# Hybrid MLA/FoX layer: the query latent's normalising factor applied inside the softmax exponential instead of to the latent

## Chip, core and metric

The kernel runs on one core of one Trainium2 chip. The metric is the device time of one execution in microseconds, as the median of several executions. Less is better.

## The reference, cut to what the change touches

One decoder layer for 512 tokens of width 2048. The layer has two kinds of attention heads; the change concerns only the eight MLA heads, whose queries come out of a normalised latent of 768 channels:

```
def _rms_norm(x, g):
    y = xf * lax.rsqrt(jnp.mean(xf * xf, axis=-1, keepdims=True) + NORM_EPS)
    return y * g
...
proj = _rms_norm(x, g_pre) @ w_in            # q_lat (768), kv_lat (512), k_rope, gates, FoX q/k/v
q = (_rms_norm(q_lat, g_q) @ w_uq)           # 8 heads x (128 nope + 64 rope)
kv = (_rms_norm(kv_lat, g_kv) @ w_ukv)
logits = (qn @ k_nope.T + rope(qr) @ rope(k_rope).T) * MLA_QK_DIM ** -0.5
p = softmax(causal(logits));  o = p @ v
...
x + _rms_norm(concat(o_mla * silu(gate), o_fox * silu(gate)) @ w_out, g_post)
```

The factor `rsqrt(mean(q_lat^2) + eps)` is one number per token, that is, one per row of the logits. It can be multiplied in before the query projection or after the scores; the result is the same up to rounding.

## The kernel before

All arithmetic is float32. A product of two float32 matrices is made of three TensorE matmuls (lines 138 to 140, `mm3`): each operand is split into a high part (ScalarE rounds it to the fast format) and a low part (VectorE subtracts the high part). Weights arrive in chunks of 128x1024 numbers, loaded by SyncE's queue into `raw`; `divide` (lines 241 to 252) splits each into `whi` on ScalarE (L250) and `wlo` on VectorE (L251). For every chunk TensorE therefore waits for a VectorE instruction of its own chunk.

The program is one long list of matmuls on TensorE, and everything else is threaded between them: small work items stand in a list `todo`, and `pump` takes one or two of them after each step of a product. `wait(n)` puts n empty items in the list. The order on each engine is then settled by the scheduler of the framework when the program is built; each engine runs its own list strictly in that order.

The stages, in the order of time: the FoX heads' projections and their attention (to about 405 us); the latents and the gates of the MLA heads, made with sums of weight blocks (to about 600 us; the products are called p1, p4, p2, q6, g5, g7, g3, their outputs in PSUM A, B, C, G, in the profile gl, gm, gc, gd); four pairs of MLA heads (to about 735 us); the output projection with its final normalisation.

**The latents.** The transposed query latent lies in six tiles of 128 channels x 512 tokens (`lat`, indices 0 to 5), the key/value latent in four more (6 to 9). `latent` squares each tile on ScalarE and adds up (L1148, L1152). `latent_stats(j)` sums over the channels with TensorE (L1162, outputs lbq and lbk), and makes the factor of each token as a column of 128x4 numbers (L1167 to L1172). `diagonals` and `latent_row` turn that column into a row that is the same in all partitions: ScalarE and VectorE make diagonal matrices (L452, L453), TensorE multiplies them by ones (L461, L462, outputs lrq and lrk) and VectorE copies the row out (L463, into `ls`). `latent_part(i)` multiplies tile i by the row and by the channel's gain (L1182) and splits the product (L129, L130, outputs `ln`).

**The MLA heads.** For each pair of heads the queries (`mq`) come from the six query latents, the keys and values (`mk`, `mv`) from the four others. The factor 192 ** -0.5 (`SC_M`) is put on the queries when they are split (L1333 to L1336). `Head.scores` makes four blocks of scores per head (`sm`, up to 128x512), adds the causal mask on VectorE (L607), takes the negated row maximum on VectorE (L620, column 0 of `st`), the exponentials on ScalarE with that as bias and the row sum as a second output (L622, output `pm`), and divides by the sum on VectorE (L623, L624). `Head.flip` transposes the blocks on TensorE (L631, `ptm`), splits them (`phm`, `plm`), and `Head.values` multiplies by the values (`pvm`).

Scores and transposes share three PSUM banks (`att_bank`): a new block of scores or transposes waits until the block three before it has been read, for scores by the exponential.

Of the kernel before, what the change touches and what calls it, by code (L numbers as in the profile page):

```python
# [19 lines left out]
P = 128  # L20
# [43 lines left out]
def tile_hybrid_layer(  # L64
# [77 lines left out]
    def newton_rsqrt(y, v, t):  # L142

        dve.tensor_tensor(out=t, in0=y, in1=v, op=ALU.mult)
        dve.tensor_tensor(out=t, in0=t, in1=y, op=ALU.mult)
        dve.tensor_scalar(out=t, in0=t, scalar1=-0.5, scalar2=1.5, op0=ALU.mult, op1=ALU.add)
        dve.tensor_tensor(out=y, in0=y, in1=t, op=ALU.mult)
# [325 lines left out]
    def wait(n):  # L473
        todo.extend([lambda: None] * n)
# [110 lines left out]
    class Head:  # L585
# [7 lines left out]
        def scores(self, b):  # L593
# [27 lines left out]
            p = pp.tile([P, n], F32, tag=f"p{b}", name=f"p{self.name}{b}")  # L621
            act.activation(p, s[:, :n], AF.Exp, bias=st[:, 0:1], accum_out=st[:, 1:2])  # L622
            dve.reciprocal(st[:, 2:3], st[:, 1:2])  # L623
# [516 lines left out]
    def raw(i):  # L1140
        return raws_of[(i // 2 + 1) % 5][:, i % 2, :]
# [11 lines left out]

    lat_diag = {}

    def latent_stats(j):
# [13 lines left out]
        dve.reciprocal(y, w)  # L1170
        newton_rsqrt(y, v, w)
        dve.tensor_tensor(out=y, in0=y, in1=rcol, op=ALU.mult)  # L1172
        lat_diag[j] = diagonals(y, f"lr{name}")
# [6 lines left out]
    def latent_part(i):  # L1180
        j = int(i >= 6)
        dve.scalar_tensor_tensor(  # L1182
            out=raw(i), in0=raw(i), scalar=gcol[:, NK + i : NK + i + 1], in1=accs[:, j, :],
            op0=ALU.mult, op1=ALU.mult,
        )
        latents[i] = split(raw(i), f"ln{i}")
# [109 lines left out]
    for i in range(4, 8):  # L1296
        todo.append(lambda i=i: latent(i, raw(i)))
    wait(2)
    todo.append(lambda: latent_stats(0))
    todo.append(lambda: latent_stats(1))  # L1300
    wait(6)
    todo.append(lambda: latent_row(0))
    todo.append(lambda: latent_row(1))
    wait(3)
    for i in range(10):
        todo.append(lambda i=i: latent_part(i))
# [21 lines left out]
    for p in range(4):  # L1328
# [3 lines left out]
        proj_T(c["q"], [(qb[i], P, cols(i * P)) for i in range(3)], qnh, qnl, rate=2)  # L1332
        q = [[split(qb[i], f"mq{p}{i}", SC_M, first=P)] for i in range(2)]  # L1333
        wholes = slot(f"mw{p}")
        qw = [[whole_block(wholes, i, qb[i], SC_M)] for i in range(2)]
        a, b = rotate(qb[2], P, SC_M, f"q{p}")  # L1336
        for i in range(2):
# [274 lines left out]
```

## Time and profile before

| | us |
|---|---|
| three runs | 909.24, 910.70, 915.02 |
| median of the three | 910.7 |
| the profiled execution, its own time | 909.88 |
| its span, first to last instruction | 908.1 |
| mean granted TensorE clock | 0.998 |

A profile row gives the start and the length in us, the engine, the line of the kernel, the operation with output and inputs by name, its shape, and in brackets the time the engine stood idle before it and what ended that. `x2` means that neighbouring instructions of one kind are merged. PE is TensorE, PEld its weight loads, DVE is VectorE, ACT is ScalarE, SPq is SyncE's queue of DMA issues. The ends of matmuls are modelled and overlap the next one's start, so distances between starts are what to read there.

### The profile page before, as it was taken

What the parts mean: (1) busy time and instruction counts of PE and PEld (TensorE: products, weight loads), DVE (VectorE), ACT (ScalarE), POOL (GpSimd) and SP (SyncE); (2) the same over time, 40 slices, a digit from 0 to 9 for tenths busy, and PEclk for the clock granted to TensorE, in tenths of its full rate; (3) what the DMA queues carried; (4) which work ended last, traced back from release to release, by engine and by line L of the source; (5) the groups of instructions that cost most, each with busy time, mean ns of one, the idle gap of its engine ahead of it and who ended that gap; (6) DMA issues with size and microseconds to landing.
All of it is one profiled execution on the core that took longest, in us unless ns stands there. A gap on an engine that the chain in (4) does not pass through costs nothing.

```text
span 908.1 us, 12914 instructions
## 1 busy us (share of the span) xinstructions
PE 897.0 (99%) x4732; PEld 773.1 (85%) x4732; DVE 634.9 (70%) x1082; ACT 423.5 (47%) x779; POOL 71.7 (8%) x89
## 2 busy tenths in 40 slices
PE   9999999999999999999999999999999999999996
PEld 8988888898889988888998998878888888888885
DVE  3477778437473683474677777978878986997785
ACT  5772434234222342242445556644455465654483
POOL 1010111110120111101000000000100000000021
PEclk9999999999999999999999999999999999999999
DMA  9378897987897987988888875548674146799888
GB/s 299 99 200 218 228 206 207 238 228 187 229 263 199 227 232 204 231 203 215 276 285 306 271 236 163 162 134 205 152 173 127 47 133 196 251 320 303 272 223 249
DMA packets 120195, 195.20 MB, mean 215 GB/s; under 512 B 15906, under 2 KB 59452, under 8 KB 120132
## 3 DMA queue, kind: packets, MB, share of 16 engines
q1 hardware_dynamic: 106052, 158.84, 55.3%
q0 software_dynamic: 13344, 35.13, 20.7%
q8 instruction: 37, 0.61, 0.3%
q10 hardware_dynamic: 736, 0.40, 0.2%
q14 instruction: 26, 0.21, 0.1%
HBM read 182.27 MB, written 62.41 MB: 269 GB/s over the span
## 4 chain that ended last, share of the span: by engine, by line
PE 91%; DVE 4%; DMA 3%; ACT 1%; issue 1%; SPq 0%; ACTq 0%; DVEq 0%
PE fv L562 4%; PE fg L138 3%; PE fq L140 3%; PE fq L138 3%; PE fq L139 3%; PE fg L140 3%; PE fg L139 3%; PE fk L138 3%; PE fk L140 3%; PE fk L139 3%; PE sm L605 3%; PE fv L138 2%; PE fv L140 2%; PE fv L139 2%; PE mq L138 2%; PE mq L140 2%
## 5 line engine op out<-in xcount | busy, mean ns | idle before, releaser
L251 DVE TENSOR_TENSOR wlo<-raw,whi 128x1024 fp32r<-128x1024 f32 (+3 forms) x205 | 242.6, 1186 | 152.5 <-ACT whi L250 148.1
L250 ACT CAST whi<-raw 128x1024 fp32r<-128x1024 f32 (+3 forms) x205 | 209.1, 1022 | 286.9 <-PE fk L139 48.3
L138 PE MATMUL fq<-h,whi 128*128 128x512 f32 x128 | 52.6, 411 | 0.0
L138 PE MATMUL fg<-h,whi 128*128 128x512 f32 x128 | 50.9, 398 | 0.0
L140 PE MATMUL fq<-h,wlo 128*128 128x512 f32 x128 | 50.3, 393 | 0.0
L140 PE MATMUL fg<-h,wlo 128*128 128x512 f32 x128 | 50.2, 392 | 0.0
L139 PE MATMUL fq<-h,whi 128*128 128x512 f32 x128 | 50.1, 391 | 0.0
L138 PE MATMUL fk<-h,whi 128*128 128x512 f32 x128 | 50.0, 391 | 0.0
L139 PE MATMUL fg<-h,whi 128*128 128x512 f32 x128 | 49.9, 390 | 0.0
L139 PE MATMUL fk<-h,whi 128*128 128x512 f32 x128 | 49.8, 389 | 0.0
L140 PE MATMUL fk<-h,wlo 128*128 128x512 f32 x128 | 49.8, 389 | 0.0
L140 PE MATMUL fv<-whi,h 128*128 128x256 f32 (+1 forms) x128 | 39.5, 309 | 0.0
L139 PE MATMUL fv<-wlo,h 128*128 128x256 f32 (+1 forms) x128 | 39.5, 309 | 0.0
L138 PE MATMUL fv<-whi,h 128*128 128x256 f32 (+1 forms) x128 | 39.5, 309 | 0.0
L562 PE MATMUL fv<-whi,h 128*128 128x456 f32 x128 | 37.7, 378 | 0.0
L295 POOL DMA_DIRECT2D t<-t x16 | 13.4, 838 | 290.1 <-DMA t<-in_w_out_dram 261.2
L622 ACT ACTIVATE pf<-sf,stf 128x128 f32<-128x128 f32 (+3 forms) x32 | 16.9, 528 | 27.1 <-DVE stf L620 27.1
L138 PE MATMUL mq<-ln,whi 128*128 128x512 f32 x72 | 28.9, 401 | 0.0
L140 PEld LDWEIGHTS fq<-h,wlo 128*128 128x128 f32 x128 | 24.0, 188 | 5.4
L140 PEld LDWEIGHTS fg<-h,wlo 128*128 128x128 f32 x128 | 24.0, 188 | 5.3
L139 PE MATMUL mq<-ln,whi 128*128 128x512 f32 x72 | 28.3, 393 | 0.0
L140 PEld LDWEIGHTS fk<-h,wlo 128*128 128x128 f32 x128 | 24.0, 188 | 5.0
(525 smaller groups left out, 2460.4 us busy)
## 6 DMA issues: line engine op xcount, KB each, us to landing
raw<-in_w_in_dram SPq DMA_DIRECT2D x80, 512.0 KB
raw<-in_w_out_dram SPq DMA_DIRECT2D x32, 512.0 KB
t<-in_w_out_dram SPq DMA_DIRECT2D x24, 512.0 KB
raw<-t SPq DMA_DIRECT2D x24, 512.0 KB
t<-t POOLq DMA_DIRECT2D x16, 512.0 KB, 7.6
awaymg<-rmg POOLq DMA_DIRECT2D x8, 512.0 KB, 8.3
t<-in_w_out_dram POOLq DMA_DIRECT2D x8, 512.0 KB, 7.9
second<-in_w_in_dram SPq DMA_DIRECT2D x8, 512.0 KB
```

What stands on the lines that cost most here:

```text
L138: pe.matmul(o, ah, bh, start=first, stop=False, **kw)
L139: pe.matmul(o, ah, bl, start=False, stop=False, **kw)
L140: pe.matmul(o, al, bh, start=False, stop=last, **kw)
L250: act.copy(hi[:, :m], raw[:, :m])
L251: dve.tensor_tensor(out=lo[:, :m], in0=raw[:, :m], in1=hi[:, :m].bitcast(F32), op=ALU.subtract)
L295: pool.dma_start(to.rearrange("p (k c) -> p k c", k=2), second, accum_op=ALU.add)
L562: pe.matmul(banks[t][:, :n], a[k][:, tss[t]], b[:, j, :], start=k == 0 and m == 0, stop=k == NK - 1 and m == 2,)
L605: pe.matmul(s[:, :nn], a[:, qs], c[:, :nn], start=(i == 0), stop=(i == len(pairs) - 1))
L622: act.activation(p, s[:, :n], AF.Exp, bias=st[:, 0:1], accum_out=st[:, 1:2])
```

## The change

The row of the query latent, its diagonals and the six multiplications by it are left out. Instead the latent tiles are multiplied by the channel's gain alone while they are split (ScalarE with the gain as a per-partition scale, VectorE with one combined instruction). The factor of each token, times `SC_M`, times the factor of the first normalisation, is kept as a column `qcol` (128x4). The exponential of an MLA block takes the column as its per-partition scale, and the negated maximum is multiplied by it first, in a new ScalarE instruction on 128x1 numbers. `SC_M` disappears from the splitting of the queries. The list of work items is reordered: the six query tiles can be split before any statistics, so they come first, and the key/value latent's statistics come before the query's.

```diff
@@ Head.scores
+            unit = 1.0
+            if self.fox is None:
+                unit = qcol[:, b : b + 1]
+                act.mul(st[:, 0:1], st[:, 0:1], unit)
-            act.activation(p, s[:, :n], AF.Exp, bias=st[:, 0:1], accum_out=st[:, 1:2])
+            act.activation(p, s[:, :n], AF.Exp, bias=st[:, 0:1], scale=unit, accum_out=st[:, 1:2])
@@ latent_stats
+        if j == 0:
+            dve.scalar_tensor_tensor(out=qcol, in0=y, scalar=SC_M, in1=rcol, op0=ALU.mult, op1=ALU.mult)
+            return
         dve.tensor_tensor(out=y, in0=y, in1=rcol, op=ALU.mult)
         lat_diag[j] = diagonals(y, f"lr{name}")
@@ latent_part
+        if j == 0:
+            latents[i] = split(raw(i), f"ln{i}", gcol[:, NK + i : NK + i + 1])
+            return
         dve.scalar_tensor_tensor(
@@ the list of work
-    todo.append(lambda: latent_stats(0))
-    todo.append(lambda: latent_stats(1))
-    wait(6)
-    todo.append(lambda: latent_row(0))
-    todo.append(lambda: latent_row(1))
-    wait(3)
-    for i in range(10):
+    todo.append(lambda: latent_stats(1))
+    for i in range(6):
+        todo.append(lambda i=i: latent_part(i))
+    todo.append(lambda: latent_row(1))
+    todo.append(lambda: latent_stats(0))
+    wait(1)
+    for i in range(6, 10):
         todo.append(lambda i=i: latent_part(i))
@@ the MLA heads
-        q = [[split(qb[i], f"mq{p}{i}", SC_M, first=P)] for i in range(2)]
+        q = [[split(qb[i], f"mq{p}{i}", first=P)] for i in range(2)]
-        qw = [[whole_block(wholes, i, qb[i], SC_M)] for i in range(2)]
-        a, b = rotate(qb[2], P, SC_M, f"q{p}")
+        qw = [[whole_block(wholes, i, qb[i])] for i in range(2)]
+        a, b = rotate(qb[2], P, 1.0, f"q{p}")
```

The change moves instructions at three places that the prediction speaks of.

First, VectorE in the second half of the latents, from the split of a late key/value latent to the low part of the third of the four chunks of the product g3 (`gc` are the gates' tiles, `lat` and `ln` the latents). Before:

```order
L251 TENSOR_TENSOR wlo_5521<-raw_5466,whi_5520 128x1024
L130 TENSOR_TENSOR ln_5505<-lat_4797,ln_5505 128x512
L130 TENSOR_TENSOR ln_5515<-lat_3743,ln_5515 128x512
L1182 SCALAR_TENSOR_TENSOR lat_3743<-lat_3743,gcol,ls 128x512
L251 TENSOR_TENSOR wlo_5543<-raw_5492,whi_5542 128x1024
L130 TENSOR_TENSOR ln_5531<-lat_3743,ln_5531 128x512
L1234 SCALAR_TENSOR_TENSOR gc_4657<-gcm_5210,ncol,gc_4657 128x512
L1234 SCALAR_TENSOR_TENSOR gc_4657<-gcm_5211,ncol,gc_4657 128x512
L1234 SCALAR_TENSOR_TENSOR gc_5463<-gcm_5210,hcol,gc_5463 128x512
L1234 SCALAR_TENSOR_TENSOR gc_5463<-gcm_5211,hcol,gc_5463 128x512
L251 TENSOR_TENSOR wlo_5568<-raw_5518,whi_5567 128x1024
```

The same stretch now, up to the same chunk:

```order
L130 TENSOR_TENSOR ln_5421<-lat_3743,ln_5421 128x512
L251 TENSOR_TENSOR wlo_5445<-raw_5398,whi_5444 128x1024
L1246 SCALAR_TENSOR_TENSOR gc_5460<-gdm_5213,hcol,gpb 128x512
L1246 SCALAR_TENSOR_TENSOR gc_5460<-gdm_5214,hcol,gpb 128x512
L251 TENSOR_TENSOR wlo_5466<-raw_5424,whi_5465 128x1024
L251 TENSOR_TENSOR wlo_5484<-raw_5442,whi_5483 128x1024
L251 TENSOR_TENSOR wlo_5502<-raw_5463,whi_5501 128x1024
L251 TENSOR_TENSOR wlo_5520<-raw_5481,whi_5519 128x1024
L1246 SCALAR_TENSOR_TENSOR gc_4658<-gcm_5211,ncol,gc_4658 128x512
L1246 SCALAR_TENSOR_TENSOR gc_4658<-gcm_5212,ncol,gc_4658 128x512
L1246 SCALAR_TENSOR_TENSOR gc_5460<-gcm_5211,hcol,gc_5460 128x512
L1246 SCALAR_TENSOR_TENSOR gc_5460<-gcm_5212,hcol,gc_5460 128x512
```

The last split of a latent now stands four chunks earlier than the gates' four instructions, and four low parts follow one another without a latent between them; the last of the earlier piece (wlo_5568) comes right behind the rows shown, as wlo_5545.

Second, TensorE where the row is made, in the first chunk of the gates' product g5 (`lrq` and `lrk` are the rows, `gdm` the product). Before:

```order
L461 MATMUL lrq<-lrqdh,ones 128x512
L138 MATMUL gdm_5212<-whi_5326,bmg_4504 128x512
L139 MATMUL gdm_5212<-wlo_5327,bmg_4504 128x512
L140 MATMUL gdm_5212<-whi_5326,bmg_4504 128x512
L138 MATMUL gdm_5213<-whi_5326,bmg_4504 128x512
L139 MATMUL gdm_5213<-wlo_5327,bmg_4504 128x512
L462 MATMUL lrq<-lrqdl,ones 128x512
```

Now:

```order
L138 MATMUL gdm_5213<-whi_5299,bmg_4505 128x512
L139 MATMUL gdm_5213<-wlo_5300,bmg_4505 128x512
L140 MATMUL gdm_5213<-whi_5299,bmg_4505 128x512
L138 MATMUL gdm_5214<-whi_5299,bmg_4505 128x512
L461 MATMUL lrk<-lrkdh,ones 128x512
L1168 MATMUL lbq<-ones,ls 128x1 x4
L139 MATMUL gdm_5214<-wlo_5300,bmg_4505 128x512
L140 MATMUL gdm_5214<-whi_5299,bmg_4505 128x512
L462 MATMUL lrk<-lrkdl,ones 128x512
```

The two matmuls of the query's row are gone; the query's statistics (lbq) have moved here, so that they no longer stand beside the key/value's.

Third, ScalarE in the last pair of heads, from the second block of scores to the seventh (`pm` are exponentials, `whi` a weight chunk). Before:

```order
L622 ACTIVATE pm_7221,stm_7219<-sm_7212,stm_7219 128x256
L129 CAST boa_7238<-boa_7238 128x512
L129 CAST boa_7307<-boa_7307 128x512
L622 ACTIVATE pm_7234,stm_7232<-sm_7225,stm_7232 128x384
L622 ACTIVATE pm_7261,stm_7259<-sm_7252,stm_7259 128x512
L622 ACTIVATE pm_7271,stm_7269<-sm_7265,stm_7269 128x128
L250 CAST whi_7311<-raw_7181 128x1024
L622 ACTIVATE pm_7290,stm_7288<-sm_7281,stm_7288 128x256
L129 CAST phm_7339<-ptm_7334 128x512
L622 ACTIVATE pm_7303,stm_7301<-sm_7294,stm_7301 128x384
```

Now, from the third block on:

```order
L626 ACTIVATE stm_7235<-stm_7235,qcol 128x1
L627 ACTIVATE pm_7237,stm_7235<-sm_7228,stm_7235,qcol 128x384
L626 ACTIVATE stm_7263<-stm_7263,qcol 128x1
L250 CAST whi_7319<-raw_7182 128x1024
L627 ACTIVATE pm_7265,stm_7263<-sm_7256,stm_7263,qcol 128x512
L626 ACTIVATE stm_7274<-stm_7274,qcol 128x1
L627 ACTIVATE pm_7276,stm_7274<-sm_7270,stm_7274,qcol 128x128
L626 ACTIVATE stm_7294<-stm_7294,qcol 128x1
L627 ACTIVATE pm_7296,stm_7294<-sm_7287,stm_7294,qcol 128x256
L626 ACTIVATE stm_7308<-stm_7308,qcol 128x1
L129 CAST phm_7348<-ptm_7343 128x512
L627 ACTIVATE pm_7310,stm_7308<-sm_7301,stm_7308,qcol 128x384
```

Each exponential has the small multiplication ahead of it and waits for it; the chunk's high part has moved ahead of the fourth block's exponential. On SyncE's queue one marker of the background sums (L300, which waits for a chunk's high part) now stands ahead of two loads of key/value weights (L235) that it stood behind.

More of the change, by code (lines that the diff above doesn't have):

```diff
@@ L1154, in tile_hybrid_layer @@
     lat_diag = {}
+    qcol = cst.tile([P, NT], F32, name="qcol")
     def latent_stats(j):
```

## The prediction

> **What bounds the kernel now.** I read the page's busy shares first, then TensorE's own waits, then the stretches of time around the latents, then the single instructions there.
>
> ```profile
> span 908.1 us, 12914 instructions
> PE 897.0 (99%) x4732; PEld 773.1 (85%) x4732; DVE 634.9 (70%) x1082; ACT 423.5 (47%) x779; POOL 71.7 (8%) x89
> ```
>
> TensorE is busy for 897 of 908 us, so only two things can shorten the program: fewer matmuls, or fewer and shorter stalls of TensorE. All the work that the change takes from VectorE and ScalarE counts only as far as TensorE waited for it.
>
> ```profile
> PE mix L1454 <- ACT scaler L1453: 1.9, 1, 1.9
> ...
> PE gdm L139 <- DVE wlo L251: 0.7, 1, 0.7
> PE gbl L140 <- DVE wlo L251: 0.5, 1, 0.5
> PE gbm L139 <- DVE wlo L251: 0.5, 1, 0.5
> ```
>
> The view of waits names one stall of TensorE inside the part that is changed: gdm, the gates' product, for a low part from VectorE, 0.7 us. The two of gbl and gbm lie before the latents' statistics, and mix at the very end; the change does not touch them. Which engine makes that low part late is shown by the busy time of two stretches (columns: stretch, its length, then PE, PEld, DVE, ACT, POOL busy):
>
> ```profile
> 541.00:563.00 22.00, 22.00 (x143) 19.90 (x141) 16.64 (x36) 13.18 (x22) 0.00 (x0) 1.00 0.57 174
> ...
> 569.30:594.30 25.00, 24.36 (x113) 19.67 (x111) 24.80 (x35) 16.79 (x22) 0.00 (x0) 1.00 0.56 163
> ```
>
> From 569.3 to 594.3 us VectorE is busy for 24.80 of 25.00 us: here, and only here, it is the bound. In the 22 us before it had 5.36 us to spare. The end of the stretch, instruction by instruction:
>
> ```profile
> 587.90 1.05 ACT L250 CAST whi<-raw 128x1024 fp32r<-128x1024 f32 x1 [1.48 <-DMA raw<-in_w_in_dram]
> ...
> 590.43 1.40 DVE L1234 SCALAR_TENSOR_TENSOR gc<-gcm,ncol,gc 128x512 f32<-128x512 f32 x2
> 591.75 1.40 DVE L1234 SCALAR_TENSOR_TENSOR gc<-gcm,hcol,gc 128x512 f32<-128x512 f32 x2
> 593.07 1.21 DVE L251 TENSOR_TENSOR wlo<-raw,whi 128x1024 fp32r<-128x1024 f32 x1
> ...
> 572.40 0.39 PE L138 MATMUL gdm<-whi,bmg 128*128 128x512 f32 x1
> 572.63 0.39 PE L139 MATMUL gdm<-wlo,bmg 128*128 128x512 f32 x1
> ...
> 593.04 0.62 PE L138 MATMUL gdm<-whi,bmg 128*128 128x512 f32 x2
> 594.33 0.50 PE L139 MATMUL gdm<-wlo,bmg 128*128 128x512 f32 x1 [0.67 <-DVE wlo L251]
> ```
>
> An undisturbed matmul of 512 columns follows the one before after 0.23 us (572.40 to 572.63). The two at 593.04 start at 593.04 and 593.27, so the next was due at 593.50 and started at 594.33: 0.83 us lost. The high part of that chunk was there at 588.95; its low part began at 593.07 only because VectorE had four gate instructions and late latent work ahead of it.
>
> **The change part by part.**
>
> *VectorE among the latents.* What goes and what stays of it, as groups (count, busy us, mean ns):
>
> ```profile
> L1182 DVE SCALAR_TENSOR_TENSOR lat<-lat,gcol,ls 128x512 f32<-128x512 f32 x10 | 7.1, 743 | 0.0
> L130 DVE TENSOR_TENSOR ln<-lat,ln 128x512 fp32r<-128x512 f32 x10 | 6.5, 682 | 0.0
> ...
> L453 DVE TENSOR_SCALAR lrqdl<-ident,lrql 128x128 fp32r<-128x128 f32 x4 | 0.9, 280 | 0.0
> L463 DVE COPY ls<-lrq 128x512 f32<-128x512 f32 x1 | 0.7, 681 | 0.0
> ```
>
> Six of the ten L1182 go: 6 x 7.1/10 = 4.3 us. With the diagonals and the copy, 4.3 + 0.9 + 0.7 = 5.9 us leave VectorE. The six low parts of the query latents become combined instructions, 743 in place of 682 ns, and move ahead of 563 us: 6 x 0.7 = 4.2 us into a stretch with 5.36 us free. The crowded stretch loses 4.3 us of L1182 and the six splits, 6 x 0.65 = 3.9 us, 8.2 of 25 us. The late low part needs 0.83 us less. Were that chunk's loading unchanged, VectorE could start it at 588.95 and end it at 590.2, 3.3 us ahead of need. **Term: 0.83 us gained.** If the moved splits used up the earlier stretch, a low part there would be late instead; 4.2 of 5.36 us leaves 1.2, and each low part is made about a chunk (2.7 us, twelve matmuls of 0.23) ahead. I take nothing for that, and 0.8 us as its worst, which would return the term.
>
> *TensorE.* The two matmuls of the query's row go.
>
> ```profile
> 557.45 0.49 PE L138 MATMUL gcm<-whi,bmq 128*128 128x512 f32 x1
> 557.78 0.40 PE L139 MATMUL gcm<-wlo,bmq 128*128 128x512 f32 x1
> ...
> 563.07 0.50 PE L461 MATMUL lrq<-lrqdh,ones 128*128 128x512 f32 x1
> 563.41 0.39 PE L138 MATMUL gdm<-whi,bmg 128*128 128x512 f32 x1
> ...
> 564.57 0.45 PE L462 MATMUL lrq<-lrqdl,ones 128*128 128x512 f32 x1
> 564.86 0.39 PE L140 MATMUL gdm<-whi,bmg 128*128 128x512 f32 x1
> ```
>
> They hold TensorE for 0.34 and 0.29 us, 0.63 together. The first matmul behind the statistics' small ones takes 0.33 in place of 0.23 us (557.45 to 557.78); with lbq moved away from lbk there are two such places in place of one: 0.10 back. **Term: 0.53 us gained.** The four matmuls of lbq are only moved.
>
> *ScalarE among the latents* loses the four diagonal multiplications (1.28 us, row below) and gets a per-channel scale in six splits; it is busy 13.18 of 22 and 16.79 of 25 us there, so this costs nothing.
>
> *ScalarE in the MLA heads.* 32 blocks get one more instruction, and 32 exponentials a second operand of 128x1. Neither stands in the trace of before. The nearest rows:
>
> ```profile
> L132 ACT ACTIVATE h<-xt,gcol x16: 680/688/690, 5.3 to 46.9; 128x512 fp32r<-128x512 f32 x16
> ...
> L129 ACT CAST phm<-ptm 128x512 fp32r<-128x512 f32 x8 | 4.7, 588 | 2.9 <-PE ptm L631 1.8 <-ACT whi L250 0.6
> ...
> 558.35 0.20 ACT L1169 ACTIVATE latq_w<-latq_v 128x4 f32<-128x4 f32 x1
> ...
> 561.52 0.18 ACT L129 CAST lrqh<-latq_y 128x4 fp32r<-128x4 f32 x1
> ...
> 561.74 1.28 ACT L452 ACTIVATE lrqdh<-ident,lrqh 128x128 fp32r<-128x128 f32 x4
> ```
>
> An operand of 128x1 costs 0.10 us (688 against 588 ns for 128x512 out of PSUM), so a multiplication of 128x1 numbers costs 0.20 + 0.10 = 0.30, and the exponential 0.10 more. A ScalarE instruction that needs the result of another starts 0.04 us after it (561.70 to 561.74). **A block's way from its maximum to its exponential grows by 0.44 us**, between 0.20 (the operands free, no gap) and 0.6 (if two instructions that depend on each other also lose their usual overlap). All 32: 14.1 us of ScalarE, from 6.4 to 19.
>
> The Trainium skill, "ScalarE: Activation LUTs", section "Step-by-step: what each stage is for", calls this scale a "free affine", while its section "What ACT_TABLE_LOAD costs" charges about 93 ns for each such operand; the trace's 0.10 agrees with the second. By the first alone the 32 blocks would cost 32 x 0.34 = 10.9 us. Its section "Rules for kernel authors" gives plain multiplications to VectorE, which speaks against where this one was put; no run yet shows the alternative here.
>
> What hides it: TensorE needs a block's bank only three blocks later. Two places (ACT rows: end of an exponential; PE rows: the first use of its bank by the block three later):
>
> ```profile
> 634.08 0.58 ACT L622 ACTIVATE pm<-sm,stm 128x384 f32<-128x384 f32 x1 [2.15 <-DVE stm L620]
> ...
> 635.33 0.60 PE L605 MATMUL sm<-mk,mq 128*128 128x256 f32 x3
> ...
> 741.64 0.58 ACT L622 ACTIVATE pm<-sm,stm 128x384 f32<-128x384 f32 x1 [0.95 <-DVE stm L620]
> ...
> 742.90 0.52 PE L605 MATMUL sm<-mk,mq 128*128 128x256 f32 x3
> ...
> 748.04 0.59 ACT L622 ACTIVATE pm<-sm,stm 128x384 f32<-128x384 f32 x1
> 748.77 0.55 PE L631 MATMUL ptm<-ident,pm 128*128 128x128 f32 x3
> ```
>
> In the first pair the margin is 635.33 - 634.66 = 0.67 us, more than 0.44; the 2.15 us that ScalarE stood idle ahead of the third block keep one block's delay from reaching the next. In the last pair it is 742.90 - 742.22 = 0.68 and then 748.77 - 748.63 = 0.14. There the 0.44 is not covered as the order was; the new order puts one matmul of the output projection more ahead of the sixth block of scores and four more between it and the seventh, 0.23 us each, which gives back part of the margin and leaves a few tenths. **Term: 0.2 us lost, from 0 to 1.**
>
> *SyncE's queue.* The marker that moved past two loads waits for a chunk's high part; behind it now wait these loads, and for them the splits of the chunks that they bring.
>
> ```profile
> 653.78 1.71 SPq L235 DMA_DIRECT2D raw<-in_w_ukv_dram  x2
> 655.54 0.34 SPq L300 DMA_DIRECT2D t<-whi  x1
> ...
> 666.77 1.05 ACT L250 CAST whi<-raw 128x1024 fp32r<-128x1024 f32 x1 [0.40 <-PE mq L139]
> ```
>
> The marker went out right behind the loads (653.78 + 1.71 = 655.49). Were it to hold them even until its old time, they would go 2 us later, and the first chunk is split 11 us after that, when ScalarE waits for TensorE and not for the load. No term; without that cover it would be 2 us.
>
> *The sum.* 0.83 + 0.53 - 0.2 = 1.2 us gained. The profiled execution took 909.88 us (span 908.1, 1.8 around it): 908.7. It was 0.8 us faster than the median of the runs shown and 0.6 slower than their fastest; 1.2 off the median gives 909.5. I predict between the two, **909.0 us**.
>
> **The rivals.**
>
> *The stall comes back as another.* Speaks for it: a chunk's high part waited 1.48 us for its load at 587.90, and loads follow the release of buffers by the same VectorE instructions; a schedule this tight has some next-late low part or load. Against it: 3.3 us of room at the stall, and VectorE that works earlier also frees the buffers earlier. Only the 0.53 us then remain, less the 0.2: 910.4 by the median.
>
> *The exponentials become the bound in the last pair of heads* (slower). Place: blocks four to eight, where the margins are 0.68 and 0.14 us. Price: 8 x 0.44 = 3.5 us if each growth adds to the next one's. It decides from 1.4 us on, where it eats the two gains. All of it: 909.88 - 1.36 + 3.5 = 912.0. For it: ScalarE has 1.05-us chunk splits between those exponentials. Against it: the order has been moved to meet it, and ScalarE still stood idle 0.95 us ahead of the third of them. With the page's free scale it would be 8 x 0.34 = 2.7 us, by the Trainium skill alone.
>
> *All 32 exponentials exposed*: 910.7 - 1.4 + 14.1 = 923.4. It needs every margin to be gone, and the first pair's 0.67 us speaks against it.
>
> *More than the sum*: stalls of one or two tenths at the beginnings of pairs go too, since ScalarE and VectorE come out of the latents earlier. I allow 1 us: 908.0.
>
> *That the change does not do what it says* can be left aside: the order shows two matmuls fewer, six L1182 fewer and 32 small multiplications more.
>
> **How the numbers follow.** My forecast 0.65, the stall that comes back 0.15, the last pair 0.10, more than the sum 0.07, all exposed 0.03. The range runs from 907.0 (the fastest run shown, 909.24, less 1.36 and nearly the extra 1 us) to 912.0 (the last pair's case). About 1% is what a measurement of this kernel can tell from no change, here 9.1 us; the gains that exist add up to less than 3 us, so only the case with everything exposed leaves that band: faster 0.01, same 0.96, slower 0.03.
>
> **What would show it.** Right: no wait of gdm for wlo at about 593 us, VectorE at 17 of 25 us in that stretch, TensorE's waits without a new row above 0.3 us, a mul of about 0.30 us and exponentials 0.10 us longer, PE with two 512-column matmuls fewer. Wrong: a stall of TensorE between 541 and 563 us, rows of sm or ptm waiting for pm, or the stall at g3 still there.

## The result, and the profile after

| | before | after |
|---|---|---|
| median of 22 runs, us | 910.84 | 908.62 |
| lowest to highest, us | 909.24 to 915.02 | 906.29 to 912.08 |
| ratio of the times | | 0.9972, 95% interval 0.9963 to 0.9982 |
| span of the profiled execution, us | 908.1 | 904.7 |

The change makes the kernel 0.28% faster, 2.5 us (0.0028 x 910.84; by the interval, 1.6 to 3.4). That is inside the 1% band that the prediction named, and about twice the 1.2 us of the forecast's sum.

The page of the changed kernel, busy time by engine:

```profile
span 904.7 us, 12931 instructions
PE 894.7 (99%) x4730; PEld 772.7 (85%) x4730; DVE 630.7 (70%) x1070; ACT 432.8 (48%) x806; POOL 71.5 (8%) x89
```

TensorE has two matmuls fewer, VectorE works 4.2 us less, ScalarE 9.3 us more. TensorE's waits, all rows of the view:

```profile
PE mix L1466 <- ACT scaler L1465: 1.9, 1, 1.9
PE xt L424 <- DMA xa<-in_x_dram: 1.5, 1, 1.5
PE gbm L139 <- DVE wlo L251: 1.1, 2, 0.7
PE warm L157 <- DVE warm L152: 1.1, 1, 1.1
```

The row of gdm is gone, and none of sm, ptm, gcm or mq has come in its place; gbm lies before the latents. The end of the product g3, where the stall was, in the changed kernel (a row of VectorE, then two of TensorE):

```profile
586.82 1.22 DVE L251 TENSOR_TENSOR wlo<-raw,whi 128x1024 fp32r<-128x1024 f32 x1
...
591.68 0.48 PE L138 MATMUL gdm<-whi,bmg 128*128 128x512 f32 x1
592.00 0.39 PE L139 MATMUL gdm<-wlo,bmg 128*128 128x512 f32 x1
```

The low part ends at 588.04 and is needed at 592.00: 4.0 us early, where before it was the last thing to come. VectorE's stretch of 25 us up to there, and its costliest groups in it:

```profile
567.00:592.00 25.00, 25.00 (x119) 20.73 (x118) 21.62 (x30) 13.93 (x17) 0.00 (x0) 1.00 0.60 179
```

```profile
L251 DVE TENSOR_TENSOR wlo<-raw,whi 128x1024 fp32r<-128x1024 f32 x9 | 10.9, 1222 | 2.7 <-ACT whi L250 2.5
L1194 DVE SCALAR_TENSOR_TENSOR lat<-lat,gcol,ls 128x512 f32<-128x512 f32 x4 | 2.9, 749 | 0.0
L130 DVE TENSOR_TENSOR ln<-lat,ln 128x512 fp32r<-128x512 f32 x4 | 2.7, 688 | 0.0
L1264 DVE SCALAR_TENSOR_TENSOR gm<-gm,gmt 128x512 f32<-128x512 f32 x3 | 2.0, 683 | 0.7 <-ACT gm L1263 0.7
```

The latents' work has gone from 7.1 + 6.5 to 2.9 + 2.7 us, 8.0 less; four of ten are left of each kind. VectorE is nevertheless busy for 21.62 us: it now waits 2.5 us for ScalarE's high parts, and nine low parts (eight before) and three gate products gm (one before) fall into the stretch. VectorE works ahead.

**Where the 2.5 us are.** Starts of five matmuls in the two profiled executions, in us:

| | before | after | difference of the stretch |
|---|---|---|---|
| first gcl (product q6) | 504.21 | 503.40 | -0.81 up to here |
| first gcm (product g7) | 550.28 | 549.47 | 0.00 |
| first mq (first pair of heads) | 599.91 | 597.24 | -1.86 |
| last pvm (heads' values) | 769.38 | 766.06 | -0.65 |
| last mix (end of the program) | 902.36 | 899.37 | +0.33 |

Up to the first gcl TensorE's list is the same in both, row for row; the last experiment shows that a difference of this size comes with the execution alone. So does the 0.33 at the end: the same stretch differs by 0.42 between two executions of the changed kernel. The change is worth 1.86 us among the latents and 0.65 us in the heads, together 2.5, which is what the ratio says. The stretch of the heads holds more than the MLA heads: the first matmul of the output projection (oa) comes at 731.51 us before, inside it. The latents were forecast at 1.36. The heads were forecast to lose 0.2 and gained. The experiments below ask for both.

In the heads the new instructions take what was costed (ScalarE, 600 to 770 us, and one block instruction by instruction):

```profile
L627 ACT ACTIVATE pm<-sm,stm,qcol 128x128 f32<-128x128 f32 (+3 forms) x32 | 19.8, 618 | 0.9
...
L626 ACT ACTIVATE stm<-stm,qcol 128x1 f32<-128x1 f32 x32 | 9.2, 291 | 18.2 <-DVE stm L620 17.7
```

```profile
738.38 0.29 ACT L626 ACTIVATE stm<-stm,qcol 128x1 f32<-128x1 f32 x1 [0.40 <-DVE stm L620]
738.71 0.68 ACT L627 ACTIVATE pm<-sm,stm,qcol 128x384 f32<-128x384 f32 x1
```

The multiplication takes 0.29 us, the exponential follows 0.04 us behind it.

### The profile page after: what moved, and what is told of

Read it like the earlier page. It is cut to its first block, busy times and chain, and to the rows that moved or that the text cites. A ratio compares the mean times of both kernels' runs of the same rounds, so it can differ in the third digit from the quotient of the medians.

```text
span 904.7 us, 12931 instructions
## 1 busy us (share of the span) xinstructions
PE 894.7 (99%) x4730; PEld 772.7 (85%) x4730; DVE 630.7 (70%) x1070; ACT 432.8 (48%) x806; POOL 71.5 (8%) x89
## 4 chain that ended last, share of the span: by engine, by line
PE 95%; DMA 2%; DVE 1%; ACT 1%; issue 0%; SPq 0%; ACTq 0%; DVEq 0%
PE fv L562 4%; PE fg L138 3%; PE fq L140 3%; PE fq L138 3%; PE fq L139 3%; PE fg L140 3%; PE fg L139 3%; PE fk L138 3%; PE fk L139 3%; PE fk L140 3%; PE sm L605 3%; PE fv L138 2%; PE fv L140 2%; PE fv L139 2%; PE mq L138 2%; PE mq L140 2%
## 5 line engine op out<-in xcount | busy, mean ns | idle before, releaser
L250 ACT CAST whi<-raw 128x1024 fp32r<-128x1024 f32 (+3 forms) x205 | 209.0, 1022 | 281.6 <-PE fk L139 52.9
```

The source lines that it names most:

```text
L250: act.copy(hi[:, :m], raw[:, :m])
```

## The experiments

Each kernel was timed beside the kernel before on the same chip; the ratio is to that. "Latents" is the stretch from the first gcm to the first mq (before 49.63, after 47.77 us), "heads" the one from the first mq to the last pvm (before 169.47, after 168.82), each out of one profiled execution.

**The row alone comes back.** The change, with the query's diagonals and row computed as before and used by nobody:

```diff
         if j == 0:
             dve.scalar_tensor_tensor(out=qcol, in0=y, scalar=SC_M, in1=rcol, op0=ALU.mult, op1=ALU.mult)
-            return
...
     for i in range(6, 10):
         todo.append(lambda i=i: latent_part(i))
+    todo.append(lambda: latent_row(0))
```

> The changed kernel with the query's row made again (diagonals, two matmuls, copy) but used by nothing. The stretch from the first matmul of gcl to the first of mq took 95.70 us before and 93.84 with the change. My theory (0.83 us of stall from VectorE's six multiplications, 0.63 us of the row's two matmuls, the rest from less broken runs): 94.5 us here, the stall at the third chunk of g3 stays away, time about 0.6 above the change's 908.6: 909.2. Rival, that VectorE's crowding by all that was removed is one thing and the row belongs to it: the stall comes back too, 95.3 or more, 910.0.

Measured 909.14 us, ratio 0.9979 (0.9968 to 0.9991); latents 48.38, heads 168.78. In this stretch the two matmuls and the diagonals cost 0.61 us, the two matmuls' own 0.63, and the stall stays away. So the stall did not hang on the diagonals and the copy. From gcl to mq, the stretch that the expectation names, it is 94.91 us: above the 94.5 of the theory and below the 95.3 of the rival. The other 0.46 us lie in the product q6, ahead of everything that comes back: a load of bmg is late there (ScalarE rounds it 22.74 us behind the first gcl, 21.06 in the change), and a low part behind it. One execution does not tell whether the edit or chance delayed that load.

**The six multiplications come back.** The change, with a multiplication by ones ahead of each query latent's split:

```diff
+    one_row = ones.unsqueeze(1).to_broadcast([P, NT, P])
...
         if j == 0:
+            dve.scalar_tensor_tensor(
+                out=raw(i), in0=raw(i), scalar=ones[:, 0:1], in1=one_row, op0=ALU.mult, op1=ALU.mult
+            )
             latents[i] = split(raw(i), f"ln{i}", gcol[:, NK + i : NK + i + 1])
```

> The changed kernel with six multiplications put back on VectorE (each query tile times ones, ahead of its split, at the new early place); the output stays the same. VectorE is busy 19.26 of 21.1 us there with the change, so 4.3 us more do not fit. My theory (VectorE's lateness is what TensorE waited for): the stretch from gcl to mq grows from 93.84 to about 94.6 us, with a wait of TensorE for a low part. Rival, that the gain is the row's matmuls and the order alone: 93.8 to 93.9.

Measured 910.55 us, ratio 1.0002 (0.9992 to 1.0011); latents 48.95, heads 168.85. The largest of the new delays, in TensorE's rows:

```profile
575.03 0.61 PE L138 MATMUL gcm<-whi,bmg 128*128 128x512 f32 x2
575.95 0.50 PE L139 MATMUL gdm<-wlo,bmg 128*128 128x512 f32 x1 [0.31 <-DVE wlo L251]
```

The two of 575.03 should have been followed at 575.48; it was 575.95, 0.47 lost, at another chunk than before. With the smaller delays, the 4.4 us more of VectorE (6 x 0.74) cost TensorE 1.18 us in this stretch; from gcl to mq it is 95.03 us, for 94.6 expected. VectorE's lateness is the price, and the place where it shows moves with the work. By the ratios this kernel is 2.7 us slower than the change (0.0030 x 910.84); each ratio has an interval of some 0.001 to either side, and where the rest lies was not found.

**The old order of the work items.** The change, with the query's splits behind the statistics again:

```diff
-    todo.append(lambda: latent_stats(1))
-    for i in range(6):
-        todo.append(lambda i=i: latent_part(i))
-    todo.append(lambda: latent_row(1))
-    todo.append(lambda: latent_stats(0))
-    wait(1)
-    for i in range(6, 10):
+    todo.append(lambda: latent_stats(0))
+    todo.append(lambda: latent_stats(1))
+    wait(7)
+    todo.append(lambda: latent_row(1))
+    wait(3)
+    for i in range(10):
         todo.append(lambda i=i: latent_part(i))
```

> The changed kernel with the old order of the work list: both statistics first, then the key row, then all ten splits. My theory (fewer instructions, wherever they stand): VectorE's crowded 25 us lose the six multiplications of 4.3 us, no stall, gcl to mq 93.8 to 94.1 us. Rival, that moving the six splits ahead is what counts: 94.5 or more, with the stall partly there.

Measured 908.78 us, ratio 0.9979 (0.9968 to 0.9991); latents 47.91, heads 168.86, no stall; gcl to mq 93.98 us, inside the range of the theory. Moving the splits ahead, which the prediction counted for 3.9 of the 8.2 us that leave the crowded stretch, is worth 0.14 us. That the instructions are fewer is what counts.

**The exponentials alone.** The kernel before, with the multiplication and the operand of the exponentials, both by a column of ones; latents and `SC_M` as before:

```diff
-            act.activation(p, s[:, :n], AF.Exp, bias=st[:, 0:1], accum_out=st[:, 1:2])
+            unit = 1.0
+            if self.fox is None:
+                unit = ones[:, 0:1]
+                act.mul(st[:, 0:1], st[:, 0:1], unit)
+            act.activation(p, s[:, :n], AF.Exp, bias=st[:, 0:1], scale=unit, accum_out=st[:, 1:2])
```

> The kernel before with only the softmax part of the change: the negated maximum times a column of ones and the exponential with that column as scale; everything else as before. From the first matmul of mq to the last of pvm it took 169.47 us before and 168.82 with the change. My theory: the 0.44 us a block are hidden, and the gain of 0.65 us in the heads is not theirs: 169.4 to 169.8 here, gcl to mq 95.7, time 910.8 to 911.2. Rival 1, that the new order around the exponentials is that gain: 168.8. Rival 2, that the exponentials are exposed in the last pair: 171 to 173, 912 to 914.

Measured 910.31 us, ratio 0.9985 (0.997 to 1.0001); latents 49.65 as before, with their stall; heads 168.90. The theory, that the gain in the heads is not that of the exponentials, is wrong, and rival 1, the new order around them, has the number: the kernel gains 0.57 us there, nearly all of what the change gains. In this kernel the order of TensorE's and VectorE's instructions in the heads is that of the change, row for row. The question became whether the order does it or the arithmetic, and the next kernels change the one with little of the other.

**An idle multiplication.** The kernel before, with a multiplication per block that nobody waits for:

```diff
+            if self.fox is None:
+                extra = pp.tile([P, 1], F32, tag="ex", name=f"ex{self.name}{b}", bufs=4)
+                act.mul(extra, st[:, 0:1], ones[:, 0:1])
             act.activation(p, s[:, :n], AF.Exp, bias=st[:, 0:1], accum_out=st[:, 1:2])
```

> The kernel before, with one more 128x1 multiplication on ScalarE in each of the 32 MLA blocks whose result nobody reads: the exponential neither waits for it nor gets an operand more, the latents stay as they were (row, six multiplications). It moves the order of TensorE's matmuls in the heads (runs of mk and mv that are whole) as the change does. Theory A (the heads' 0.65 us comes from that new order alone): first mq to last pvm takes 168.8 to 169.0 us in place of 169.47, the stretch gcl to mq stays at 95.7, time 910.2 to 910.6 beside 910.9 of before. Theory B (it comes from the exponentials, whose result is ready at another time): 169.3 to 169.6 in the heads, time 910.9 or, with 32 x 0.3 us more on ScalarE, somewhat longer.

Measured 911.31 us, ratio 1.0 (0.9982 to 1.0017); heads 169.73. Neither theory's number: its heads are slower than before. The order that the scheduler made for it is a third one; the expectation was wrong to take it for that of the change. Its rows led to the two places below.

**A constant in place of the column.** The kernel before, with `SC_M` moved from the queries into the softmax as a number:

```diff
+            unit = 1.0
+            if self.fox is None:
+                unit = SC_M
+                act.mul(st[:, 0:1], st[:, 0:1], unit)
-            act.activation(p, s[:, :n], AF.Exp, bias=st[:, 0:1], accum_out=st[:, 1:2])
+            act.activation(p, s[:, :n], AF.Exp, bias=st[:, 0:1], scale=unit, accum_out=st[:, 1:2])
...
```

> The kernel before, with only the constant 1/sqrt(192) taken out of the queries and put into the softmax as a number in the instruction: a 128x1 multiplication by it and the exponential's scale, no 128x1 operands. Latents as before (95.7 us from gcl to mq, a stall of gdm of about 0.8). Theory A (order alone): heads 168.8 to 169.1 us, time 910.2 to 910.6. Theory B (per-token operand): heads 169.4 or more. On ScalarE I expect the exponential at about 530 ns (as before, since the number costs nothing) against 618 with the operand, and the multiplication at 0.20 us against 0.29; that would say that the operands cost 0.09 us each.

Measured 911.46 us, ratio 1.0003 (0.9986 to 1.0019); heads 169.83, latents as before. Its groups on ScalarE:

```profile
L626 ACT ACTIVATE pm<-sm,stm 128x128 f32<-128x128 f32 (+3 forms) x32 | 16.9, 527 | 0.9
...
L625 ACT ACTIVATE stm<-stm 128x1 f32<-128x1 f32 x32 | 6.3, 201 | 21.5 <-DVE stm L620 21.2
```

A column as operand costs 0.09 us on either instruction (618 against 527 ns, 291 against 201); a number costs nothing. The Trainium skill, "ScalarE: Activation LUTs", section "What ACT_TABLE_LOAD costs", has about 93 ns for it, and the trace agrees; the same page's "free affine" holds here for the number, not for the column. The 169.83 us of the heads lie in theory B's range and outside theory A's, but again the order is one of its own, so neither could be tested with it.

**The two places.** The heads of before and after differ mainly at two places of TensorE, 0.35 and 0.19 of the 0.65 us. The first is the values of the third pair, between the products of the fourth pair's queries. Before:

```profile
696.62 0.47 PE L138 MATMUL mq<-ln,whi 128*128 128x512 f32 x1
696.66 0.95 DVE L251 TENSOR_TENSOR wlo<-raw,whi 128x768 fp32r<-128x768 f32 x1
...
697.02 0.39 PE L138 MATMUL pvm<-phm,mv1h 128*128 128x256 f32 x1
...
697.53 0.42 DVE L130 TENSOR_TENSOR plm<-ptm,phm 128x256 fp32r<-128x256 f32 x1
697.71 0.40 PE L138 MATMUL mq<-ln,whi 128*128 128x512 f32 x1
...
698.00 0.19 PEld L139 LDWEIGHTS pvm<-plm,mv1h 128*128 128x128 f32 x1 [0.34 <-DVE plm L130]
698.01 0.39 PE L139 MATMUL pvm<-plm,mv1h 128*128 128x256 f32 x1
```

After:

```profile
693.89 0.48 PE L138 MATMUL mq<-ln,whi 128*128 128x512 f32 x1
...
694.11 0.42 DVE L130 TENSOR_TENSOR plm<-ptm,phm 128x256 fp32r<-128x256 f32 x1
...
694.21 0.31 PE L138 MATMUL pvm<-phm,mv1h 128*128 128x256 f32 x1
...
694.82 0.28 PE L139 MATMUL pvm<-plm,mv1h 128*128 128x256 f32 x1
...
695.33 0.95 DVE L251 TENSOR_TENSOR wlo<-raw,whi 128x768 fp32r<-128x768 f32 x1
```

Before, VectorE makes a chunk's low part (0.95 us) and then plm, and the matmul on plm waits until 698.01. After, plm stands ahead of the low part and is there early. Around this product, what the distances of starts exceed 0.23 us (512 columns) or 0.12 us (256) by adds up to 0.44 us before and 0.1 after. The second place is the fourth pair's values product mv, whose bank VectorE frees with the last rbq. Before:

```profile
719.33 2.11 DVE L819 SCALAR_TENSOR_TENSOR rbq<-mq,sinT 32x512 f32<-32x512 f32 x3
...
721.18 0.40 PE L140 MATMUL mk<-ln,wlo 128*128 128x512 f32 x1
...
721.49 0.19 PEld L138 LDWEIGHTS mv<-whi,ln 128*128 128x128 f32 x1 [0.34 <-DVE rbq L819]
721.49 0.39 PE L138 MATMUL mv<-whi,ln 128*128 128x256 f32 x1
721.72 0.28 PE L139 MATMUL mv<-wlo,ln 128*128 128x256 f32 x1
```

After, TensorE is further from the end of rbq:

```profile
715.89 2.80 DVE L824 SCALAR_TENSOR_TENSOR rbq<-mq,sinT 32x512 f32<-32x512 f32 x4
...
718.12 0.39 PE L140 MATMUL mk<-ln,wlo 128*128 128x512 f32 x1
718.35 0.28 PE L138 MATMUL mv<-whi,ln 128*128 128x256 f32 x1
718.47 0.28 PE L139 MATMUL mv<-wlo,ln 128*128 128x256 f32 x1
```

Here 0.31 and 0.23 us stand against 0.23 and 0.12, 0.19 lost before and nothing after: those at 718.35 start before rbq ends at 718.69, so they do not need it, and those that do must come later in TensorE's list. Both are matters of order on VectorE and TensorE, and no exponential is in them.

**The order kept, idle work added.** The kernel before, with two idle multiplications per block that depend on nothing; the order of all other instructions in the heads is exactly that of before:

```diff
+            if self.fox is None:
+                extra = pp.tile([P, 1], F32, tag="ex", name=f"ex{self.name}{b}", bufs=4)
+                act.mul(extra, ones[:, 0:1], ones[:, 0:1])
+                act.mul(extra, ones[:, 0:1], ones[:, 0:1])
             act.activation(p, s[:, :n], AF.Exp, bias=st[:, 0:1], accum_out=st[:, 1:2])
```

> The kernel before, with two more 128x1 multiplications on ScalarE in each of the 32 MLA blocks that depend on no block at all (ones by ones); in the heads the order of all other instructions on TensorE, VectorE and ScalarE is exactly that of before. Theory 'order' (the heads' time follows from the order of the instructions and not from what ScalarE has to do): first mq to last pvm again 169.4 to 169.6 us as before, though ScalarE works 32 x 2 x 0.29 = 19 us more; time within 0.5 us of before. Rival 'load': with more work on ScalarE the heads go as slowly as in the kernel with one idle multiplication (169.76) or slower, by up to 19 us.

Measured 920.69 us, ratio 1.0103 (1.0082 to 1.0124). Against the expectation it is 10 us slower, and the profile shows why: the scheduler put all 64 at the very start. One of the two groups, by first and last start, and TensorE's longest wait:

```profile
L624 ACT ACTIVATE exm<-ones x32: 278/281/284, 4.5 to 18.2; 128x1 f32<-128x1 f32 x32
```

```profile
PE fv L562 <- ACT whi L250: 6.5, 1, 6.5
```

The heads, with the order of before, take 169.46 us (before 169.47). That says that the same order gives the same time in another execution; since the load was not in the heads, the rival "load" is not tested by it. The other side of this: in the kernels with the row back, the six multiplications, the old work order and the exponentials alone, and in the change once more, TensorE's and VectorE's instructions in the heads stand in the order of the change, and all five took 168.78 to 168.90 us. All of them have the longer way too, so this does not separate order and exponentials.

**The operand alone, and the multiplication alone.** The kernel before, with one half of the addition each; the first changes `scale`, the second puts the multiplication by ones ahead of the exponential:

```diff
-            act.activation(p, s[:, :n], AF.Exp, bias=st[:, 0:1], accum_out=st[:, 1:2])
+            act.activation(p, s[:, :n], AF.Exp, bias=st[:, 0:1], scale=(ones[:, 0:1] if self.fox is None else 1.0), accum_out=st[:, 1:2])
```

> The kernel before, with a 128x1 operand of ones as the scale of the 32 exponentials and no multiplication: each exponential about 0.09 us longer, the order in the heads nearly that of before (one matmul of mq, six of mv and one of oa change places, and some instructions of VectorE in the last pair). Theory 'order': 169.2 to 169.6 us in the heads, as before. Rival 'operand' (the longer exponential by itself makes the heads shorter): 168.8 to 169.0.

```diff
+            if self.fox is None:
+                act.mul(st[:, 0:1], st[:, 0:1], ones[:, 0:1])
             act.activation(p, s[:, :n], AF.Exp, bias=st[:, 0:1], accum_out=st[:, 1:2])
```

> The kernel before, with one 128x1 multiplication by ones between the maximum and the exponential, and the exponential without the operand: the way grows by 0.33 us. The order of TensorE in the heads is nearly that of the change (three matmuls of mq and some of mv stand elsewhere). Theory 'order': 168.7 to 169.2 us in the heads, as with the change, latents as before (95.7), so about 910.3 us. Rival 'operand': 169.4 or more.

The operand: 909.93 us, ratio 0.9995 (0.9982 to 1.0008), heads 169.20. The multiplication: 911.7 us, ratio 1.0004 (0.999 to 1.0017), heads 169.16, latents 49.65. For both kernels theory "order" named a range that holds the heads' time at its edge, and rival "operand" one that does not hold it. The times of the whole cannot tell 0.3 us; the heads' stretches can, and the table shows what they follow:

| kernel | a block's way grows by | heads, us | lost at the two places | heads less this |
|---|---|---|---|---|
| before | 0 | 169.47 | 0.44 + 0.19 | 168.84 |
| after | 0.42 | 168.82 | 0.09 + 0 | 168.73 |
| exponentials alone | 0.42 | 168.90 | 0.09 + 0 | 168.81 |
| operand alone | 0.09 | 169.20 | 0.29 + 0.07 | 168.84 |
| multiplication alone | 0.33 | 169.16 | 0.28 + 0 | 168.88 |
| idle multiplication | 0 | 169.73 | 0.42 + 0.28, and 0.21 at mv of two earlier pairs | 168.82 |
| constant | 0.24 | 169.83 | 0.43 + 0.28, 0.21 at mv, 0.11 at a block of scores | 168.80 |

The last column is the same for all within 0.15 us: in these seven, what differs is how long pvm waits for phm and plm, and mv for rbq. It does not follow the growth of the way from maximum to exponential. That the order makes these waits is read from the rows; what stays open is the direct test: before's arithmetic under exactly the change's order could not be had, since the scheduler makes the order from the instructions. The two kernels that follow lose time at other places as well.

**Six times the multiplication.** The change, with five more by ones in each block:

```diff
                 act.mul(st[:, 0:1], st[:, 0:1], unit)
+                for _ in range(5):
+                    act.mul(st[:, 0:1], st[:, 0:1], ones[:, 0:1])
```

> The change, with five more 128x1 multiplications (by ones) on ScalarE in each of the 32 MLA blocks, between the maximum and the exponential: each 0.29 us and 0.04 us until the next, so the way grows by 5 x 0.33 = 1.65 us beside the change and by 2.1 us beside before; ScalarE gets 46 us more. Theory 'covered up to a margin' (margins of 0.68 us at the third-next block): the part beyond the margin, about 1.4 us, shows at the blocks where TensorE has nothing else, some two or three of a pair: 4 pairs x 2 x 1.4 = 11 us at most, less what the new order gives back; I expect 911 to 917 us with rows of sm or ptm that wait for pm. Rival 'never on the path' (TensorE always has other matmuls): within 0.5 us of the change. Rival 'every growth adds' : 908.6 + 32 x 1.65 = 961 us.

Measured 910.86 us, ratio 0.9998 (0.9981 to 1.0014), about 2.4 us slower than the change; heads 170.71, 1.89 more. The added group, and the largest wait that comes with it:

```profile
L628 ACT ACTIVATE stm<-stm,ones 128x1 f32<-128x1 f32 x160 | 39.1, 288 | 0.8
```

```profile
PE pvm L138 <- ACT phm L129: 0.4, 1, 0.4
```

46 us more on ScalarE (160 x 0.288) cost TensorE 1.9 us. "Covered up to a margin" has the direction but too large a number, and mainly the wrong place. The weight loads of scores and transposes do wait for exponentials now (three of sm, 0.6 us in all, and two of ptm, 0.6), but loads run ahead of the matmuls, and the scores' own starts lose under 0.1 us. What TensorE waits for is phm, which ScalarE makes behind a chunk's high part (L250, 732.23 to 733.29), and plm behind it.

**The multiplication on VectorE.** The change, with

```diff
-                act.mul(st[:, 0:1], st[:, 0:1], unit)
+                dve.tensor_scalar(out=st[:, 0:1], in0=st[:, 0:1], scalar1=unit, scalar2=None, op0=ALU.mult)
```

> The change, with the 128x1 multiplication given to VectorE, which has just made the maximum, in place of ScalarE. The way from maximum to exponential gets shorter by one change of engine or by nothing; both theories of the heads expect 168.6 to 169.0 us there as long as TensorE waits for neither engine. Theory 'hidden' (the 0.44 us that each block's way grew is covered): 908.2 to 909.2 us, no difference from the change that can be measured. Rival (the growth was exposed in the last pair by some tenths): 0.3 to 1.0 us faster than the change. VectorE: 32 instructions of 0.1 to 0.2 us more.

Measured 908.24 us, ratio 0.9974 (0.9959 to 0.999), against 0.9972 of the change: no difference that these intervals can show. Its heads took 169.49 us, so the range of 168.6 to 169.0 was missed, and here the exponentials are exposed. In the first pair, at the place where the prediction read its first margin:

```profile
632.16 0.67 ACT L627 ACTIVATE pm<-sm,stm,qcol 128x384 f32<-128x384 f32 x1 [2.08 <-DVE stm L626]
...
632.97 0.42 PEld L605 LDWEIGHTS sm<-mk,mq 128*128 128x128 f32 x3 [0.21 <-ACT pm L627]
632.98 0.62 PE L605 MATMUL sm<-mk,mq 128*128 128x256 f32 x3
```

The exponential ends at 632.83 and the scores that use its bank come 0.27 us late. In the change the same exponential ends at 632.17 and the scores start at 632.63: 0.46 us to spare, where before had 0.67. In the last pair five more weight loads of sm and ptm wait for exponentials, and from the first oa to the last pvm TensorE takes 38.10 us (37.81 in the change). The third block's maximum comes 0.60 us later than in the change, behind a chunk's low part that waits 0.49 us for its high part. The multiplication itself is shorter on VectorE:

```profile
L626 DVE TENSOR_SCALAR stm<-stm,qcol x32: 195/207/215, 626.5 to 746.5; 128x1 f32<-128x1 f32 x32
```

207 against 291 ns. The rule of the Trainium skill that the prediction weighed ("ScalarE: Activation LUTs", "Rules for kernel authors": plain multiplications to VectorE) thus gives the shorter instruction here, and nothing that the time shows.

**The change once more**, unaltered:

> The change once more, unaltered: it tells which differences between two profiled executions belong to the program and which to the execution. Theory 'order': the stretches where TensorE is not fed late repeat to 0.1 us, gcm to mq 47.8 and the heads 168.8 us, while the time until gcl (503.4 in the first profile of the change, 504.2 before) comes out anywhere between 503 and 506, since all kernels so far lie there whatever they change. Rival 'the start belongs to the change': again 503.4 within 0.2. Time 908.0 to 909.5 us.

Measured 909.22 us, ratio 0.9972 (0.9961 to 0.9983), the same as the first time. Latents 47.77 and heads 168.89, as in the first profile to 0.07 us; but the first gcl starts at 506.72 in place of 503.40, beyond even the 503 to 506 that were named. Of the 3.3 us, 2.4 are lost at one late load:

```profile
463.27 1.22 DVE L247 TENSOR_TENSOR raw<-raw,second 128x1024 f32<-128x1024 f32 x1 [2.35 <-DMA second<-in_w_in_dram]
...
465.68 0.58 PE L140 MATMUL gbl<-h,wlo 128*128 128x256 f32 x1 [2.34 <-DVE wlo L251]
```

So the first row of the table of stretches (0.81 us) is within what two executions of one program differ by, and the latents and the heads belong to the program.

## Why the prediction was right, and where its numbers were off

The time lay where it was forecast, and its main mechanism, a low part that VectorE brings late among the latents, was the right one. That 909.0 comes within 0.4 us of the 908.62 measured is in part luck: the gain was forecast 1.3 us too small, and the time that it was taken from (909.0 + 1.2 = 910.2) was 0.6 below the median of 910.84. By its own steps:

**VectorE among the latents (0.83 us gained).** Right; it was 0.94: with the stall the longer distance behind it went too (594.33 to the next at 594.67, 0.11 over 0.23). The needed chunk's part came 4.0 us early, for 3.3 forecast. That the crowded stretch would show 17 of 25 busy us was wrong, though 8.0 of the forecast 8.2 us did leave it: the free time was filled by work that moved up. VectorE, relieved, worked ahead, so its busy share in the window did not measure what had been taken away. The stall that was feared in the stretch before did not come (VectorE is busy 19.26 of 21.10 us there, from 540.20 on, and TensorE waits for no low part).

**TensorE (0.53).** The two matmuls were worth their 0.63; the 0.10 back for lbq's separation did not come. The small matmuls now (first two rows, then the one behind) and before:

```profile
562.47 0.94 PE L1168 MATMUL lbq<-ones,ls 128*128 128x1 f32 x8
563.27 0.48 PE L139 MATMUL gdm<-wlo,bmg 128*128 128x512 f32 x1
563.59 0.40 PE L140 MATMUL gdm<-whi,bmg 128*128 128x512 f32 x1
```

```profile
555.75 0.94 PE L1162 MATMUL lbq<-ones,ls 128*128 128x1 f32 x8
556.56 1.03 PE L1162 MATMUL lbk<-ones,ls 128*128 128x1 f32 x8
557.45 0.49 PE L138 MATMUL gcm<-whi,bmq 128*128 128x512 f32 x1
```

A second 0.32 us does follow lbq (563.27 to 563.59). But side by side, the second eight had taken 0.89 us (556.56 to 557.45) where lbq takes 0.80 alone, so the 0.1 had been paid before as well. **The term should have been 0.63.** This step counted one side of a move only.

**What the latents gave besides**: 0.2 us. In g3 the gates' transposes (gmt) stand in four groups in place of five, and each group costs the matmul behind it some 0.1 us (591.68 to 592.00 for 0.23). It comes from the new order, and no step had counted it. 0.94 + 0.63 + 0.2, with some hundredths, make the 1.86.

**The heads (0.2 lost, 0 to 1).** This step failed. The costs were right: 0.29 us for the forecast 0.30, 0.09 for 0.10, 0.04 for 0.04. The place named, the last pair, lost nothing: from the first oa to the last pvm TensorE took 37.87 us before and 37.81 after. Of the gain of 0.65, 0.54 lay at two places that the prediction did not look at. The view of waits that it shows is that of matmuls (PE); the same view for weight loads (PEld), from 690 to 770 us, names both in the kernel before (pvm for plm 0.5 us, mv for rbq 0.3) and neither in the changed one. The 32 longer blocks are covered in the changed kernel: the exponentials alone, on before's latents, give 168.90 us. That the gain comes from the order that the scheduler makes is what the table of the two places says; it was not isolated. The prediction had read the new order only where it feared a loss. Its fear was not idle: with the multiplication on VectorE, scores and transposes do wait for exponentials, in the first pair and in the last.

**SyncE's marker (no term).** Right as far as the waits go: the changed kernel has no wait of TensorE for a weight in the heads.

**The rivals.** The stall did not come back. The last pair of heads was not the bound, and the 32 exponentials were not all exposed: even where each block's way grows by five times as much (2.1 us) the heads lose 1.9 us in all. "More than the sum" (908.0) is the nearest of them; its direction was right, its reason, that the engines come out of the latents earlier, was not, since the kernel with the exponentials alone has the gain with the old latents.

## What to carry to other kernels

Before a change is credited with what follows a small instruction, compare the order of all engines over the whole stage, not only where a loss is feared: with the blocks' way 0.42 us longer, the scheduler put one split ahead of another and some matmuls ahead of those that wait, and 0.54 us of waiting went. Read the waits of weight loads as well as those of matmuls. Where the bounding engine is relieved, price the relief by the stalls that it had caused, not by its busy share. And compare stretches between landmarks rather than whole spans where a term is below the scatter of the executions: the two stretches here repeat to 0.1 us, the whole differs by 3.8.

## What the runs showed of the hardware

A load that came late set TensorE back by 2.3 us in one execution of a program and not in another, before anything that the change touches; of the 3.8 us between the two profiled executions of the change (899.37 and 903.18 at the last matmul of the mix), 3.3 arose before the first gcl. A column of 128x1 numbers as scale costs an activation 0.09 us, whether it works on one element per partition (201 against 291 ns) or on 128 to 512 (527 against 618 ns on average), and a number as scale costs nothing (527 ns with it and without).
